# A hybrid encoder layer on one core: the second block product of the gate and up projections by quarter blocks, four products chained in one PSUM bank

## The chip, the cores and the metric

One core of a Trainium2 chip runs the whole layer as one launch. Its five engines work through queues of their own: TensorE (PE, with its weight loads PEld), VectorE (DVE), ScalarE (ACT), GpSimd (POOL) and SyncE (SP, which issues the DMAs). The metric is the device time in microseconds (us), from which the median of several runs is taken.

## The reference, cut to what matters

```python
u = x @ w_in                                  # retention heads, windowed attention heads
h = layer_norm(alpha * x + concat(R, A) @ w_out)
g, up = h @ w_ffn_gate, h @ w_ffn_up          # 1024 x 1024 by 1024 x 2816, twice
ffn = (silu(g) * up) @ w_ffn_down
out = layer_norm(alpha * h + ffn + sigmoid(h @ w_ple_gate) * (p @ w_ple_proj))
```

All of it is float32, and 1024 tokens run through one layer. The change lies in the lines of `g`, `up` and `silu(g) * up`.

## The kernel before, in words

Every float32 operand of a matmul is split into a high and a low part (`split`: ACT rounds, DVE subtracts), and a product is made of three matmuls (`mm3c`, lines 783 to 785: high by high, high by low, low by high).

Gate and up have 22 hidden blocks of 128 columns, taken as 11 pairs. For a pair n, with m = 0 the gate weights and m = 1 the up weights, the 256 hidden columns by 1024 inner by 1024 tokens are a 2 by 2 by 2 block product. It is done with seven products instead of eight (Strassen's scheme in Winograd's form). `RIGHT[p]` holds the token side of product p, ready split; the weight side is loaded as `raw` and `ln` tiles, summed where the scheme asks for it (`s_sums`), and split into an operand tile. A unit is one product p for one m: four steps of the inner size by three matmuls, 12 matmuls of 512 columns, into one bank. A pair has 14 units. The products go to three banks per m: X takes products 1 and 2, Y takes 6, 7 and 4, Z takes 5 and 3. `post` reads the banks and adds up the four output blocks c11, c12, c21 and c22; each has its gate half put through Silu (`finish`, m = 0) and multiplied by its up half (`finish`, m = 1). `asum` then forms the differences of the blocks that the down projection wants, and they are stored in `ad`.

The order on PE, DVE, ACT, POOL and SP is the order in which the code emits it (`manual_schedule`). The loop over the units emits for each the matmuls (`mm`), then `post`, and then `ahead(2, ...)`, which prepares (`prep`) operands for up to 8 units further on. Each engine works off its queue in that order, save that a PE weight load can run beside the matmul before it; an instruction that waits holds back all that stands behind it. In the kernel before, DVE makes the low parts and the sums that read a bank; POOL makes the weight sums (lines 1187 to 1191), the products with the Silu halves (line 1217) and the differences (line 1221). Operand tiles rotate through four tiles `w` and four tiles `u`, the eight PSUM banks through four names (`mm`, `s`, `t`, `o`) of two banks each.

Of the kernel before, what the change touches and what calls it, by code (L numbers as in the profile page):

```python
# [9 lines left out]
F32 = mybir.dt.float32  # L10
# [32 lines left out]
def layer(tc, xT, xn, w_first, w_mt, w_rv, w_out, w_pg, w_pe, pT, w_gu, w_dn,  # L43
# [26 lines left out]
    def split(raw, hi, lo):  # L70
        act.activation(hi, raw, AF.Copy)  # L71
        dve.tensor_tensor(lo, raw, hi.bitcast(F32), ALU.subtract)  # L72
# [699 lines left out]
    def ct(shape, tag, bufs=None, dt=F32):  # L772
        return cpool.tile(list(shape), dt, tag=tag, bufs=bufs, name=nm(tag))
# [7 lines left out]
    def mm3c(o, lh, ll, rh, rl, start, stop):  # L781

        pe.matmul(o, lh, rh, start=start, stop=False, skip_group_check=True)  # L783
        pe.matmul(o, lh, rl, start=False, stop=False, skip_group_check=True)  # L784
        pe.matmul(o, ll, rh, start=False, stop=stop, skip_group_check=True)  # L785
# [375 lines left out]
    sarena = arena8  # L1161
    ptags = ("mm", "s", "t", "o")

    def pair_tile():
        return a_tile([P, 2, HF], "ev")

    stores = []

    class Pair:
# [10 lines left out]
                for j in range(2):  # L1180
                    self.raw[m, i, j] = r[:, j * HF:(j + 1) * HF]

        def s_sums(self, m, part=(0, 1)):
            a = lambda i, j: self.raw[m, i, j]
            s = self.s[m] = [sarena[:, 4 * m + k, :] for k in range(4)]
            if 0 in part:
                pool.tensor_tensor(s[1], a(1, 0), a(1, 1), ALU.add)  # L1187
                pool.tensor_tensor(s[0], s[1], a(0, 0), ALU.subtract)  # L1188
            if 1 in part:
# [3 lines left out]
        def prep(self, p, m, k):  # L1193
            src = {1: lambda: self.raw[m, 0, 0], 2: lambda: self.raw[m, 0, 1], 4: lambda: self.raw[m, 1, 1],
                   5: lambda: self.s[m][1], 6: lambda: self.s[m][0], 7: lambda: self.s[m][2],
                   3: lambda: self.s[m][3]}[p]()
            t = wp.tile([P, 2, HF], F32R, tag="w", bufs=4, name=nm("w")) if k % 2 == 0 else ct([P, 2, HF], "u", 4, F32R)
            split(src, t[:, 0, :], t[:, 1, :])
            self.ops[p, m] = t

        def mm(self, p, m):
            g = {1: 0, 2: 0, 6: 1, 7: 1, 4: 1, 5: 2, 3: 2}[p]
            first = p in (1, 6, 5)
            if first:
                self.bank[g, m] = bank(ptags[(3 * self.n + g) % 4])
            b, w, r = self.bank[g, m], self.ops[p, m], RIGHT[p]
            for kt in range(4):
                c = slice(kt * P, (kt + 1) * P)
                mm3c(b, w[:, 0, c], w[:, 1, c], r[:, 0, kt, :], r[:, 1, kt, :], first and kt == 0, kt == 3)

        def finish(self, name, m):

            c = self.ev[name]
            if m == 0:
                act.activation(c[:, 0, :], c[:, 0, :], AF.Silu)  # L1215
            else:
                pool.tensor_tensor(c[:, 1, :], c[:, 0, :], c[:, 1, :], ALU.mult)  # L1217

        def asum(self, dst, left, right, op):

            pool.tensor_tensor(self.ev[dst][:, 0, :], left, right, op)  # L1221

        def post(self, p, m, k):
            ev, X, Y, Z = self.ev, self.bank.get((0, m)), self.bank.get((1, m)), self.bank.get((2, m))

            def get(name):
                if m == 0:
                    ev[name] = pair_tile()
                return ev[name][:, m, :]

            def add(name, left, right):
                dve.tensor_tensor(get(name), ev[left][:, m, :], right, ALU.add)  # L1232

            a = lambda name: ev[name][:, 1, :]
            s = lambda name: ev[name][:, 0, :]
            wait = 2 if self.n < NP - 1 else 8
            if p == 1:
                act.activation(get("s1"), X, AF.Copy)
            elif p == 6:
                add("u2", "s1", Y)  # L1240
            elif p == 2:
                c = get("c11")
                if m == 0:
                    act.activation(c, X, AF.Silu)
                else:
                    dve.tensor_tensor(c, ev["c11"][:, 0, :], X, ALU.mult)
            elif p == 7:
                add("u3", "s1", Y)
                add("c22", "u3", Z)
                self.finish("c22", m)  # L1250
            elif p == 4:
                add("c21", "s1", Y)
                self.finish("c21", m)
                if m:
                    self.asum("c21", a("c21"), a("c11"), ALU.subtract)
                    stores.append((k + wait, lambda: sp.dma_start(ad[self.n, 2, :, 0, :], s("c21"))))
                    self.asum("c11", s("c21"), a("c22"), ALU.subtract)
                    stores.append((k + wait, lambda: sp.dma_start(ad[self.n, 0], ev["c11"])))
                    self.asum("c22", a("c22"), a("c21"), ALU.subtract)
                    stores.append((k + wait, lambda: sp.dma_start(ad[self.n, 3], ev["c22"])))  # L1260
            elif p == 3:
                add("c12", "u2", Z)
# [9 lines left out]
    def g_unit(n, p, m, k):  # L1272
        pr = pairs2[n]

        def prep():
            if p == 1 and n:
                pr.load(m)
            pr.prep(p, m, k)
            if p == 1:
                if n:  # L1280
                    pr.s_sums(m)
                else:
                    pr.s_sums(m, (0,))
                    if m:
                        pr.s_sums(0, (1,))
                        pr.s_sums(1, (1,))

        return prep, lambda: pr.mm(p, m), lambda: pr.post(p, m, k)
# [323 lines left out]

    ET = mybir.EngineType
    with tc.manual_schedule(engines={ET.PE, ET.DVE, ET.Activation, ET.Pool, ET.SP}):
        ahead(2, 4)
        for k in range(NG):
            gunits[k][1]()
            gunits[k][2]()
            ahead(2, k + 1 + min(8, 4 + k))
# [106 lines left out]
```

## Time and profile before

| what | value |
|---|---|
| runs | 1180.26 us median of 3 (1179.91 to 1180.78) |
| the profiled execution | 1180.62 us, of which the span of the instructions 1178.8 us |
| granted PE clock | 0.997 |
| PE, PEld busy | 99%, 82% of the span |
| DVE, ACT, POOL busy | 65%, 45%, 31% of the span |
| gate and up | from 540 us to about 960 us of the span |

A busy PE in this profile means that a matmul is under way, and matmuls overlap: one of 512 columns is listed with 0.39 us, but the next starts long before that is over. The rate is read from the starts in the timeline. An engine's idle time counts only where it ends in a wait of PE.

### The profile page before, as it was taken

How to read it: one execution, taken by the hardware profiler on the slowest of the kernel's cores; microseconds unless marked ns; L12 is line 12 of the kernel's file. 1: busy time of each engine (PE TensorE's matmuls, PEld its weight loads, DVE VectorE, ACT ScalarE, POOL GpSimd, SP SyncE). 2: the span in 40 equal slices, each digit the busy share in tenths (PEclk: the TensorE clock that was granted, in tenths of full speed). 3: DMA queues.
4: the chain of work that ended last, by engine and by line, in shares of the span. 5: the costliest groups of instructions: out<-in, count | busy, mean ns of one | idle time of the engine just before them, and what ended most of it. 6: DMA issues, size and time to landing. Idle time of an engine off the chain costs nothing.

```text
span 1178.8 us, 17058 instructions
## 1 busy us (share of the span) xinstructions
PE 1167.3 (99%) x6068; PEld 968.4 (82%) x6068; DVE 767.3 (65%) x1310; ACT 534.4 (45%) x1049; POOL 365.5 (31%) x346
## 2 busy tenths in 40 slices
PE   9999999999999999999999999999999999999996
PEld 7888888888888888888788888888888888888885
DVE  5566678776849688948655455545555465774777
ACT  5566348777756265214332333323333325563463
POOL 2001010202010020004765647464655341134242
PEclk9999999999999999999999999999999999999998
DMA  6345656545346955665323331233213179999977
GB/s 253 107 148 215 241 182 240 188 152 205 123 151 240 361 186 195 242 221 176 124 76 120 134 110 70 90 134 135 77 63 129 72 221 323 354 270 229 258 164 208
DMA packets 80661, 211.71 MB, mean 180 GB/s; under 512 B 9536, under 2 KB 14784, under 8 KB 80576
## 3 DMA queue, kind: packets, MB, share of 16 engines
q1 hardware_dynamic: 71936, 193.84, 46.2%
q0 software_dynamic: 8640, 16.78, 8.0%
q8 instruction: 48, 0.79, 0.3%
q14 instruction: 37, 0.30, 0.1%
HBM read 139.29 MB, written 62.13 MB: 171 GB/s over the span
## 4 chain that ended last, share of the span: by engine, by line
PE 94%; DVE 3%; ACT 1%; issue 1%; DMA 1%; DVEq 0%; SPq 0%; ACTq 0%
PE bmm L77 6%; PE bs L785 6%; PE bs L783 6%; PE bs L784 6%; PE bmm L79 6%; PE bmm L78 6%; PE bt L783 5%; PE bt L785 5%; PE bt L784 5%; PE bmm L785 5%; PE bmm L783 5%; PE bmm L784 5%; PE bo L785 5%; PE bo L783 5%; PE bo L784 5%; PE bo L565 2%
## 5 line engine op out<-in xcount | busy, mean ns | idle before, releaser
L77 PE MATMUL bmm<-H,w 128*128 128x512 f32 x240 | 97.2, 405 | 0.2 <-ACT H L71 0.2
L79 PE MATMUL bmm<-H,w 128*128 128x512 f32 x240 | 94.1, 392 | 0.0
L78 PE MATMUL bmm<-H,w 128*128 128x512 f32 x240 | 94.0, 392 | 0.0
L1187 POOL TENSOR_TENSOR H<-ln 128x512 f32<-128x512 f32 x22 | 28.9, 1312 | 180.2 <-ACT w L71 96.1
L1217 POOL TENSOR_TENSOR ev<-ev 128x512 f32<-128x512 f32 x33 | 55.4, 1679 | 90.6 <-DVE ev L1232 63.6
L72 DVE TENSOR_TENSOR w<-H,w 128x512 fp32r<-128x512 f32 x44 | 41.6, 945 | 62.7 <-ACT w L71 62.7
L72 DVE TENSOR_TENSOR w<-raw,w 128x512 fp32r<-128x512 f32 x56 | 46.3, 832 | 47.3 <-ACT w L71 47.1
L526 POOL COPY sc<-skb 128x1 f32<-128x1 f32 x64 | 14.8, 240 | 182.5 <-PE bt L553 162.5
L1215 ACT ACTIVATE ev<-ev 128x512 f32<-128x512 f32 x33 | 20.9, 632 | 103.5 <-DVE ev L1232 103.5
L1221 POOL TENSOR_TENSOR ev<-ev,ev 128x512 f32<-128x512 f32 x44 | 62.7, 1436 | 2.6
L72 DVE TENSOR_TENSOR u<-H,u 128x512 fp32r<-128x512 f32 x47 | 38.0, 809 | 36.6 <-ACT u L71 36.2
L77 PEld LDWEIGHTS bmm<-H,w 128*128 128x128 f32 x240 | 45.1, 188 | 10.3 <-ACT H L71 1.1
L79 PEld LDWEIGHTS bmm<-H,w 128*128 128x128 f32 x240 | 45.0, 188 | 10.0
L78 PEld LDWEIGHTS bmm<-H,w 128*128 128x128 f32 x240 | 45.2, 188 | 7.8
L71 ACT ACTIVATE u<-H 128x512 fp32r<-128x512 f32 x47 | 29.6, 630 | 43.3 <-POOL H L1188 11.1
L535 ACT ACTIVATE sc<-sc,st 128x385 f32<-128x385 f32 (+1 forms) x64 | 37.2, 584 | 17.1 <-DVE st L533 17.0
L71 ACT ACTIVATE w<-raw 128x512 fp32r<-128x512 f32 x56 | 34.5, 623 | 18.8 <-PE bmm L79 6.9
L531 DVE CUSTOM_DVE_ANT_0 sc<-cst,bs,skb 128x384 f32<-128x384 f32 (+1 forms) x64 | 34.9, 577 | 9.2 <-PE bs L530 7.9
L493 POOL TENSOR_TENSOR sm<-sm,cst 128x8 f32<-128x8 f32 x8 | 13.8, 1727 | 79.9 <-DVE sm L492 79.9
L894 POOL TENSOR_TENSOR stt<-stt,cst 128x1 f32<-128x1 f32 x8 | 12.2, 1520 | 83.8 <-DVE stt L893 83.8
L1191 POOL TENSOR_TENSOR H<-raw,H 128x512 f32<-128x512 f32 x22 | 37.3, 1697 | 0.0
L71 ACT ACTIVATE w<-H 128x512 fp32r<-128x512 f32 x44 | 27.3, 621 | 21.0 <-PE bs L785 6.3
(813 smaller groups left out, 3756.2 us busy)
## 6 DMA issues: line engine op xcount, KB each, us to landing
ad<-ev SPq DMA_DIRECT2D x33, 512.0 KB, 2.6
pgd<-pro SPq DMA_DIRECT2D x28, 512.0 KB, 3.0
raw<-in_w_gu SPq DMA_DIRECT2D x22, 512.0 KB, 4.5
ln<-in_w_gu SPq DMA_DIRECT2D x22, 512.0 KB, 3.6
raw<-ad SPq DMA_DIRECT2D x40, 256.0 KB, 5.5
ln<-ad SPq DMA_DIRECT2D x37, 256.0 KB, 6.4
H<-in_w_dn SPq DMA_DIRECT2D x33, 256.0 KB, 6.6
wod<-aq SPq DMA_DIRECT2D x15, 512.0 KB, 2.7
```

The lines of the kernel that those rows point to most:

```text
L71: act.activation(hi, raw, AF.Copy)
L72: dve.tensor_tensor(lo, raw, hi.bitcast(F32), ALU.subtract)
L77: pe.matmul(o, lh, rh, start=start, stop=False)
L78: pe.matmul(o, lh, rl, start=False, stop=False)
L79: recent[0] = pe.matmul(o, ll, rh, start=False, stop=stop).ins.name
L535: act.activation(sc[g][:, :nk + 1], sc[g][:, :nk + 1], AF.Exp, bias=st_[:, 1, j, g:g + 1], accum_out=st_[:, 2, j, g:g + 1])
L783: pe.matmul(o, lh, rh, start=start, stop=False, skip_group_check=True)
L784: pe.matmul(o, lh, rl, start=False, stop=False, skip_group_check=True)
L785: pe.matmul(o, ll, rh, start=False, stop=stop, skip_group_check=True)
L1191: pool.tensor_tensor(s[3], a(0, 1), s[0], ALU.subtract)
L1217: pool.tensor_tensor(c[:, 1, :], c[:, 0, :], c[:, 1, :], ALU.mult)
L1221: pool.tensor_tensor(self.ev[dst][:, 0, :], left, right, op)
```

## The change

From the third pair on (`FROM = 2`), product 2 of both m is no longer two units of 12 matmuls. Its weight side (m by two halves of the inner size) and its token side (`RIGHT[2]`, two halves of the inner size by two halves of 256 tokens) are cut once more, and the product is done as seven quarter products by the same scheme: 7 by 2 by 3 = 42 matmuls of 256 columns instead of 24 of 512. They come in three parts, which the text calls F0 (quarter products 1, 6 and 5), F1 (7 and 2) and F2 (4 and 3), woven between the units of products 1, 6 and 5: (1,0), (1,1), F0, (6,0), F1, (6,1), F2, (5,0), (5,1), (7,0), (7,1), (4,0), (4,1), (3,0), (3,1), where (p,m) is product p for that m. The quarter products share two banks, in halves of 256 columns; `post_fine` has DVE add the halves into c11 after each part, and F1 accumulates on top of halves that F0 wrote. The token side of the quarter products (`fine_right`) is summed and split once, during the first two pairs.

In all pairs, products 1, 6, 7 and 4 now accumulate in one bank W per m, and ACT copies the bank between them (`s1`, `u2`, `u3`; the fourth goes through Silu or a multiplication straight from the bank). The sums `add("u2", ...)`, `add("u3", ...)` and `add("c21", ...)` on DVE are gone. All that POOL computed in this stage, the weight sums, the products with the Silu halves and the differences, stands on DVE. Operand tiles are taken from a list of eight and given back after the matmuls that read them (`take_op`, `free_op`); F0 needs three at once, so `ahead` stops while fewer are free.

```diff
+    Q = HF // 2
+    FINE = ((1, 6, 5), (7, 2), (4, 3))
+    FROM = 2
...
+        def prep(self, p, m):
             a = lambda i, j: self.raw[m, i, j]
-            s = self.s[m] = [sarena[:, 4 * m + k, :] for k in range(4)]
-                pool.tensor_tensor(s[1], a(1, 0), a(1, 1), ALU.add)
-                pool.tensor_tensor(s[0], s[1], a(0, 0), ALU.subtract)
-                pool.tensor_tensor(s[2], a(0, 0), a(1, 0), ALU.subtract)
-                pool.tensor_tensor(s[3], a(0, 1), s[0], ALU.subtract)
...
+            if p == 6:
+                dve.tensor_tensor(s[1], a(1, 0), a(1, 1), ALU.add)
+                dve.tensor_tensor(s[0], s[1], a(0, 0), ALU.subtract)
...
+            t = self.ops[p, m] = take_op()
             split(src, t[:, 0, :], t[:, 1, :])
+            if p == 5:
+                dve.tensor_tensor(s[2], a(0, 0), a(1, 0), ALU.subtract)
+                dve.tensor_tensor(s[3], a(0, 1), s[0], ALU.subtract)
...
+        def mm_fine(self, part):
+            if part == 0:
+                self.fb = [bank(ptags[(3 * self.n + 1) % 4]) for _ in range(2)]
+            for q in FINE[part]:
...
+                for kt in range(2):
+                    c = slice(c0 + kt * P, c0 + (kt + 1) * P)
+                    mm3c(o, t[:, 0, c], t[:, 1, c], hi[:, kt, :], lo[:, kt, :], q in (1, 5) and kt == 0, kt == 1)
...
+        def post_fine(self, part):
...
+            if part == 0:
+                add(c12, v[:, 0, Q:], bx)
+                add(low, v[:, 1, :].rearrange("p (j c) -> p j c", j=2), twice(bx))
+                add(c12, c12, by)
+            elif part == 1:
+                add(low, low, twice(by))
+                add(c22, c22, bz)
+                add(c11, v[:, 0, :Q], bx)
+            else:
+                add(c12, c12, bz)
+                add(c21, c21, bw)
+                self.finish("c11", 0)
+                self.finish("c11", 1)
...
         def mm(self, p, m):
-            g = {1: 0, 2: 0, 6: 1, 7: 1, 4: 1, 5: 2, 3: 2}[p]
-            first = p in (1, 6, 5)
+            g = {1: 0, 6: 0, 7: 0, 4: 0, 2: 1, 5: 2, 3: 2}[p]
+            first = p in (1, 2, 5)
...
         def finish(self, name, m):
...
-                pool.tensor_tensor(c[:, 1, :], c[:, 0, :], c[:, 1, :], ALU.mult)
+                dve.tensor_tensor(c[:, 1, :], c[:, 0, :], c[:, 1, :], ALU.mult)
...
         def asum(self, dst, left, right, op):
-            pool.tensor_tensor(self.ev[dst][:, 0, :], left, right, op)
+            dve.tensor_tensor(self.ev[dst][:, 0, :], left, right, op)
...
             elif p == 6:
-                add("u2", "s1", Y)
+                act.activation(get("u2"), W, AF.Copy)
...
             elif p == 7:
-                add("u3", "s1", Y)
-                add("c22", "u3", Z)
+                act.activation(get("u3"), W, AF.Copy)
+                add("c22", "u3", Z, "u3")
...
-        for p in (1, 6, 5, 2, 7, 4, 3) if n else (1, 2, 6, 5, 7, 4, 3):
+        for p in (1, 6, 5, 7, 4, 3) if n >= FROM else (1, 2, 6, 5, 7, 4, 3):
             for m in range(2):
+                if n >= FROM and p == 6:
+                    gunits.append(f_unit(n, m))
                 gunits.append(g_unit(n, p, m, len(gunits)))
+            if n >= FROM and p == 6:
+                gunits.append(f_unit(n, 2))
...
-        while done[what] < min(upto, len(units)):
+        while done[what] < min(upto, len(units)) and (what < 2 or units[done[2]][3] <= len(oslots)):
```

What moves on DVE is seen at the place where one pair hands over to the next, from the last sums of products 4 and 3 to the first sums of the next pair. The rows below are DVE's queue of the kernel before at that place, in order; each is line, operation, output and inputs, partitions by elements. `ev` tiles hold blocks, a name that starts with `b` is a bank, and line 72 is the low part of an operand.

```order
L1232 TENSOR_TENSOR ev1029_7152<-ev1005_6963,bo1009_6986 128x512
L72 TENSOR_TENSOR w1030_7155<-H697_4542,w1030_7155 128x512
L1232 TENSOR_TENSOR ev1029_7152<-ev1005_6963,bo1012_7004 128x512
L72 TENSOR_TENSOR u1031_7175<-H697_4542,u1031_7175 128x512
L1232 TENSOR_TENSOR ev1032_7190<-ev1010_6999,bt1014_7021 128x512
L72 TENSOR_TENSOR w1033_7193<-raw1019_7067,w1033_7193 128x512
L1232 TENSOR_TENSOR ev1032_7190<-ev1010_6999,bt1016_7037 128x512
L72 TENSOR_TENSOR u1034_7211<-raw1022_7091,u1034_7211 128x512
L72 TENSOR_TENSOR w1037_7232<-H697_4542,w1037_7232 128x512
L72 TENSOR_TENSOR u1039_7249<-H697_4542,u1039_7249 128x512
L1232 TENSOR_TENSOR ev1041_7266<-ev1036_7230,bmm1040_7253 128x512
```

After each unit stood one bank sum and one low part: the two sums of c21, the two of c12, and then the first of the next pair's u2.

The kernel after, DVE, at the same place: from the multiplication of c21 (line 1367, bank `bo883`) on. Line 1335 is `asum`, lines 1227 and 1228 are the weight sums of product 6, line 1243 is a sum of a quarter product, line 1346 a bank sum.

```order
L1367 TENSOR_TENSOR ev829_5336<-ev829_5336,bo883_6741 128x512
L1335 TENSOR_TENSOR ev829_5336<-ev829_5336,ev823_5330 128x512
L1335 TENSOR_TENSOR ev823_5330<-ev829_5336,ev825_5332 128x512
L1335 TENSOR_TENSOR ev825_5332<-ev825_5332,ev829_5336 128x512
L1227 TENSOR_TENSOR H697_4542<-ln887_6819 128x512
L1228 TENSOR_TENSOR H697_4542<-H697_4542,raw882_6739 128x512
L72 TENSOR_TENSOR u811_5318<-H697_4542,u811_5318 128x512
L1243 TENSOR_TENSOR cst_367<-raw882_6739,raw884_6759 128x256
L72 TENSOR_TENSOR u817_5324<-cst_367,u817_5324 128x256
L1346 TENSOR_TENSOR ev824_5331<-ev824_5331,bs889_6858 128x512
L1227 TENSOR_TENSOR H697_4542<-ln888_6823 128x512
L1228 TENSOR_TENSOR H697_4542<-H697_4542,raw884_6759 128x512
```

Eight operations now stand between the multiplication that follows unit (4,1) and the sum that follows unit (3,0), where one low part stood between two bank sums before.

The kernel after, DVE, further on in the same hand-over, after seven rows that are left out here: from the low part of operand (5,0) to the three sums after F0 (line 1295, bank `bo895`).

```order
L72 TENSOR_TENSOR w814_5321<-H697_4542,w814_5321 128x512
L1234 TENSOR_TENSOR H697_4542<-raw882_6739,ln887_6819 128x512
L1235 TENSOR_TENSOR H697_4542<-raw882_6739,H697_4542 128x512
L72 TENSOR_TENSOR u815_5322<-H697_4542,u815_5322 128x512
L1234 TENSOR_TENSOR H697_4542<-raw884_6759,ln888_6823 128x512
L1235 TENSOR_TENSOR H697_4542<-raw884_6759,H697_4542 128x512
L1295 TENSOR_TENSOR ev827_5334<-ev826_5333,bo895_7044 128x256
L1295 TENSOR_TENSOR ev827_5334<-ev826_5333,bo895_7044 128x512
L1295 TENSOR_TENSOR ev827_5334<-ev827_5334,bo895_7044 128x256
```

The weight sums for products 7 and 3 (lines 1234 and 1235) stand ahead of the sums of F0, which F1 on PE waits for.

More of the change, by code (lines that the diff above doesn't have):

```diff
@@ L1162, in layer, with take_op, free_op, fine_right @@
     ptags = ("mm", "s", "t", "o")
-    def pair_tile():
-        return a_tile([P, 2, HF], "ev")
+    Q = HF // 2
+    FINE = ((1, 6, 5), (7, 2), (4, 3))
+    FROM = 2
+    evs, nev = [], [0]
+    oslots = []
+    fright, fsum = {}, []
+    def pair_tile():
+        nev[0] += 1
+        return evs[(nev[0] - 1) % len(evs)]
+    def take_op():
+        return oslots.pop(0)
+    def free_op(t):
+        oslots.append(t)
+    def fine_right(R):
+        x = cst[:, 0:HF].rearrange("p (k c) -> p k c", k=2)
+        def blk(i, j, part):
+            return R[:, part, 2 * i:2 * i + 2, j * Q:(j + 1) * Q]
+        def both(left, right):
+            dve.tensor_tensor(x, blk(*left, 0).bitcast(F32), blk(*right, 0).bitcast(F32), ALU.subtract)
+            dve.tensor_tensor(x, x, blk(*left, 1).bitcast(F32), ALU.add)
+            dve.tensor_tensor(x, x, blk(*right, 1).bitcast(F32), ALU.subtract)
+        def less(left):
+            dve.tensor_tensor(x, blk(*left, 0).bitcast(F32), x, ALU.subtract)
+            dve.tensor_tensor(x, x, blk(*left, 1).bitcast(F32), ALU.add)
+        for q, (i, j) in {1: (0, 0), 2: (1, 0), 3: (1, 1)}.items():
+            fright[q] = blk(i, j, 0), blk(i, j, 1)
+        other = a_tile([P, 2, 2, Q], "fine", dt=F32R)
+        fright[7] = other[:, 0], other[:, 1]
+        fright[5] = tuple(ct([P, 2, Q], "sg", 2, F32R) for _ in range(2))
+        fright[6] = tuple(ct([P, 2, Q], "p", 2, F32R) for _ in range(2))
+        fright[4] = blk(0, 1, 0), blk(0, 1, 1)
+        return [lambda: (both((1, 1), (0, 1)), split(x, *fright[7])), lambda: (both((0, 1), (0, 0)), split(x, *fright[5])),
+                lambda: (less((1, 1)), split(x, *fright[6])), lambda: (less((1, 0)), split(x, *fright[4]))]
     stores = []
@@ L1193, in prep @@
[L1193 to L1197, printed above, removed]
-            split(src, t[:, 0, :], t[:, 1, :])
-            self.ops[p, m] = t
+            s = self.s.setdefault(m, [sarena[:, 4 * m + k, :] for k in range(4)])
@@ new lines, in prep_fine, with sum_, put @@
+        def prep_fine(self, part):
+            x, y = (self.raw[m, 0, 1] for m in range(2))
+            left = {1: x[:, :Q], 2: x[:, Q:], 4: y[:, Q:], 5: fsum[0], 6: fsum[1], 7: fsum[2], 3: fsum[3]}
+            def sum_(q, a, b, op):
+                dve.tensor_tensor(left[q], a, b, op)
+            def put(t, h, q):
+                c = slice(h * Q, (h + 1) * Q)
+                split(left[q], t[:, 0, c], t[:, 1, c])
+                self.fine[q] = t, h * Q
+            if part == 0:
+                self.fine = {}
+                t, u, v = (take_op() for _ in range(3))
+                self.fu = u
+                sum_(5, y[:, :Q], y[:, Q:], ALU.add)
+                sum_(6, left[5], x[:, :Q], ALU.subtract)
+                split(x, t[:, 0, :], t[:, 1, :])
+                self.fine.update({1: (t, 0), 2: (t, Q)})
+                put(u, 0, 5)
+                put(v, 0, 6)
+            elif part == 1:
+                sum_(7, x[:, :Q], y[:, :Q], ALU.subtract)
+                put(self.fu, 1, 7)
+            else:
+                w = take_op()
+                sum_(3, x[:, Q:], left[6], ALU.subtract)
+                put(w, 0, 4)
+                put(w, 1, 3)
@@ new lines, in mm_fine @@
+        def mm_fine(self, part):
+            if part == 0:
+                self.fb = [bank(ptags[(3 * self.n + 1) % 4]) for _ in range(2)]
+            for q in FINE[part]:
+                t, c0 = self.fine[q]
+                i, j = {1: (0, 0), 2: (0, 0), 6: (0, 1), 7: (0, 1), 5: (1, 0), 3: (1, 0), 4: (1, 1)}[q]
+                o = self.fb[i][:, j * Q:(j + 1) * Q]
+                hi, lo = fright[q]
+                for kt in range(2):
+                    c = slice(c0 + kt * P, c0 + (kt + 1) * P)
+                    mm3c(o, t[:, 0, c], t[:, 1, c], hi[:, kt, :], lo[:, kt, :], q in (1, 5) and kt == 0, kt == 1)
+            for q in ((6,), (7, 2), (4,))[part]:
+                free_op(self.fine[q][0])
@@ new lines, in post_fine, with add, twice @@
+        def post_fine(self, part):
+            ev = self.ev
+            if part == 0:
+                ev["c11"] = pair_tile()
+            o, v = ev["c11"], ev["s1"]
+            (c11, c12), (c21, c22) = ([o[:, m, j * Q:(j + 1) * Q] for j in range(2)] for m in range(2))
+            (bx, by), (bz, bw) = ([b[:, j * Q:(j + 1) * Q] for j in range(2)] for b in self.fb)
+            low = o[:, 1, :].rearrange("p (j c) -> p j c", j=2)
+            def add(out_, x, y):
+                dve.tensor_tensor(out_, x, y, ALU.add)
+            def twice(b):
+                return b.unsqueeze(1).to_broadcast([P, 2, Q])
+            if part == 0:
+                add(c12, v[:, 0, Q:], bx)
+                add(low, v[:, 1, :].rearrange("p (j c) -> p j c", j=2), twice(bx))
+                add(c12, c12, by)
+            elif part == 1:
+                add(low, low, twice(by))
+                add(c22, c22, bz)
+                add(c11, v[:, 0, :Q], bx)
+            else:
+                add(c12, c12, bz)
+                add(c21, c21, bw)
+                self.finish("c11", 0)
+                self.finish("c11", 1)
@@ L1261, in post @@
             elif p == 3:
-                add("c12", "u2", Z)
+                add("c12", "u2", Z, "u2")
                 self.finish("c12", m)
@@ L1275, in prep, with f_unit @@
         def prep():
[L1276 to L1288, printed above, removed]
+            pr.prep(p, m)
+            if n + 1 < NP and p in (5, 4):
+                pairs2[n + 1].load(m, ((0,), (1,))[p == 4])
+        return prep, lambda: pr.mm(p, m), lambda: pr.post(p, m, k), 1
+    def f_unit(n, part):
+        pr = pairs2[n]
+        return lambda: pr.prep_fine(part), lambda: pr.mm_fine(part), lambda: pr.post_fine(part), (3, 0, 1)[part]
     for n in range(NP):
-        for p in (1, 6, 5, 2, 7, 4, 3) if n else (1, 2, 6, 5, 7, 4, 3):
+        for p in (1, 6, 5, 7, 4, 3) if n >= FROM else (1, 2, 6, 5, 7, 4, 3):
             for m in range(2):
+                if n >= FROM and p == 6:
+                    gunits.append(f_unit(n, m))
                 gunits.append(g_unit(n, p, m, len(gunits)))
+            if n >= FROM and p == 6:
+                gunits.append(f_unit(n, 2))
     LASTS = [(0, 1, "mm"), (1, 1, "s"), (2, 1, "mm"), (3, 1, "s"), (4, 1, "mm"), (4, 0, "s"), (5, 1, "mm"), (5, 0, "s"),
@@ L1614, in layer @@
     with tc.manual_schedule(engines={ET.PE, ET.DVE, ET.Activation, ET.Pool, ET.SP}):
+        for _ in range(4):
+            oslots.append(wp.tile([P, 2, HF], F32R, tag="w", bufs=4, name=nm("w")))
+            oslots.append(ct([P, 2, HF], "u", 4, F32R))
+        fine = fine_right(RIGHT[2])
+        evs.extend(a_tile([P, 2, HF], "ev") for _ in range(7))
+        fsum.extend([cst[:, 0:Q], cst[:, Q:2 * Q], cst[:, 2 * Q:3 * Q], ct([P, Q], "fs", 1)])
         ahead(2, 4)
```

37 lines of the change are left out of this document (19 added, 18 removed).

## The prediction

> **What bounds the kernel now.** I read the page first, for the shares and the chain that ended last:
>
> ```profile
> span 1178.8 us, 17058 instructions
> ...
> PE 1167.3 (99%) x6068; PEld 968.4 (82%) x6068; DVE 767.3 (65%) x1310; ACT 534.4 (45%) x1049; POOL 365.5 (31%) x346
> ...
> PE 94%; DVE 3%; ACT 1%; issue 1%; DMA 1%; DVEq 0%; SPq 0%; ACTq 0%
> ```
>
> PE is busy almost throughout, and the chain runs through PE. The waits of PE tell whether it ever stood still for gate and up. The columns are who waited for whom, us in total, times, longest:
>
> ```profile
> PE bs L783 <- DVE ev L1232: 0.7, 1, 0.7
> ```
>
> One wait of 0.7 us belongs to this stage (it lies at 570 us). A stretch in the middle of the stage, by windows (busy us and instructions of PE, PEld, DVE, ACT, POOL, then the granted clock):
>
> ```profile
> 650.00:700.00 50.00, 50.00 (x222) 41.39 (x222) 27.23 (x33) 15.97 (x28) 31.35 (x21) 1.00 0.30 110
> ```
>
> PE never idles, DVE is busy for 27 us of 50, POOL for 31. So the stage ends when PE has issued its matmuls; the other engines have slack, and the reader should note how much of DVE's slack the change uses.
>
> The rate of PE comes from the starts in its timeline (start, duration). Fourteen steps of 512 columns lie between these two rows:
>
> ```profile
> 699.69 0.39 PE L785 MATMUL bs<-H,w 128*128 128x512 f32 x1
> ...
> 702.87 0.39 PE L784 MATMUL bs<-H,u 128*128 128x512 f32 x1
> ```
>
> (702.87 - 699.69) / 14 = 0.227 us for each. A unit of 12 is 2.73 us, a pair of 14 units 38.15 us.
>
> **The change on PE.** No matmul of 256 columns stands in this stage, but some in attention:
>
> ```profile
> 330.36 0.28 PE L530 MATMUL bs<-kz,aq 128*128 128x256 f32 x1
> 330.47 0.28 PE L529 MATMUL bs<-k,aq 128*128 128x256 f32 x1
> 330.59 0.28 PE L530 MATMUL bs<-kz,aq 128*128 128x256 f32 x1
> 330.71 0.39 PE L77 MATMUL bmm<-H,w 128*128 128x512 f32 x1
> ```
>
> Three steps take 0.35 us, 0.117 us each. 24 matmuls of 0.227 (5.45 us) become 42 of 0.117 (4.91 us): 0.54 us a pair, 4.9 us over the nine pairs. [...]
>
> So an unhindered pair is 12 units and 42 quarter matmuls, 32.7 + 4.9 = 37.6 us.
>
> **The change on DVE.** What an operation costs there, from its timeline:
>
> ```profile
> 553.23 1.78 DVE L72 TENSOR_TENSOR w<-H,w 128x512 fp32r<-128x512 f32 x1
> 554.94 0.68 DVE L72 TENSOR_TENSOR u<-H,u 128x512 fp32r<-128x512 f32 x1
> ...
> 560.34 0.68 DVE L72 TENSOR_TENSOR u<-H,u 128x512 fp32r<-128x512 f32 x1
> ...
> 566.14 0.67 DVE L1232 TENSOR_TENSOR ev<-ev,bs 128x512 f32<-128x512 f32 x1
> 566.85 0.69 DVE L1232 TENSOR_TENSOR ev<-ev,bmm 128x512 f32<-128x512 f32 x1
> ```
> ```profile
> 551.00:554.90 3.90, 3.85 (x17) 2.87 (x16) 3.90 (x3) 2.90 (x6) 3.47 (x3) 1.00 0.72 164
> 554.90:560.90 6.00, 6.00 (x29) 4.95 (x28) 6.00 (x11) 1.35 (x3) 0.00 (x0) 1.00 0.35 102
> ```
>
> The nine steps from 554.94 to 560.34, through a full queue with POOL still (0.00 in the second window), are 0.60 us each. At 553.23 POOL computes too (3.47 of 3.90), and one takes 1.78. Where an operation reads what the one before it wrote (the last two rows), the step is 0.71. POOL gives up these:
>
> ```profile
> L1187 POOL TENSOR_TENSOR H<-ln 128x512 f32<-128x512 f32 x22 | 28.9, 1312 | 180.2 <-ACT w L71 96.1
> L1217 POOL TENSOR_TENSOR ev<-ev 128x512 f32<-128x512 f32 x33 | 55.4, 1679 | 90.6 <-DVE ev L1232 63.6
> L1221 POOL TENSOR_TENSOR ev<-ev,ev 128x512 f32<-128x512 f32 x44 | 62.7, 1436 | 2.6
> ```
>
> With three more lines of weight sums like the first they are 15 operations a pair. On DVE each costs 0.60 instead of 1.3 to 1.7 us, and the contention of 1.78 goes. Half-width rows, for the quarter products, with ACT's beside it:
>
> ```profile
> L431 DVE COPY kv<-bt 128x256 f32<-128x256 f32 x4 | 1.7, 425 | 3.7 <-PE bt L423 3.7
> L429 ACT ACTIVATE kv<-bt 128x256 f32<-128x256 f32 x4 | 1.5, 372 | 0.5 <-DVE kv L431 0.5
> ```
>
> A half-width DVE step is then about 0.34 us (0.425 less the 0.08 by which a full one overlaps the next). A pair's DVE queue grows from 25 operations to 35 full and 15 half: 35 x 0.60 + 15 x 0.34 = 26.1 us of 37.6, 69%. On average it fits. It doesn't fit where it is bunched.
>
> **The hand-over.** Count from the moment at which PE has issued unit (4,1) and starts (3,0). Until F1 of the next pair, PE has (3,0), (3,1), (1,0), (1,1), F0 and (6,0): five units and 18 quarter matmuls, 13.6 + 2.1 = 15.7 us. F1 adds onto halves of a bank that the three sums after F0 must have read. In the queue of DVE these stand behind everything in the order rows of the change. What a hand-over between engines costs:
>
> ```profile
> 701.73 0.39 PE L785 MATMUL bs<-H,w 128*128 128x512 f32 x1
> 702.16 0.69 DVE L1232 TENSOR_TENSOR ev<-ev,bs 128x512 f32<-128x512 f32 x1 [0.88 <-PE bs L785]
> 702.88 0.69 DVE L72 TENSOR_TENSOR w<-ln,w 128x512 fp32r<-128x512 f32 x1
> 696.72 0.60 ACT L1238 ACTIVATE ev<-bt 128x512 f32<-128x512 f32 x1 [2.03 <-PE bt L785]
> 697.22 0.62 ACT L71 ACTIVATE w<-H 128x512 fp32r<-128x512 f32 x1
> 697.87 1.32 DVE L72 TENSOR_TENSOR w<-H,w 128x512 fp32r<-128x512 f32 x1 [1.76 <-ACT w L71]
> ```
>
> PE's last matmul starts at 701.73, DVE goes on at 702.16: 0.43 later, 0.2 us after the start of the next unit. ACT's rounding ends at 697.84, the subtraction starts 0.03 later. So a weight sum that is split at once holds DVE for 0.69 + 0.03 + 0.62 + 0.03 = 1.37 us before the low part can start. Walking down DVE's queue (start of the next operation, us):
>
> - c21 times up, three differences, the two weight sums of (6,0): 0.2 + 3 x 0.72 + 2 x 0.60 + 1.37 = 4.9
> - low part, the sum and low part of quarter product 7, with ACT's half-width 0.37 between: 0.60 + 0.85 + 0.45, to 6.8
> - c12 after (3,0), the sums of (6,1), low part: 0.60 + 0.72 + 1.37 + 0.60, to 10.1
> - c12 after (3,1), its multiplication, a difference: 0.72 + 0.72 + 0.60, to 12.2
> - F2's sum and low parts: 0.85, to 13.0; then 1.17 in which ACT copies s1 and rounds (5,0), to 14.2
> - low parts and weight sums of (5,0) and (5,1): 4 x 0.60 + 2 x 0.72 = 3.8, to 18.0
> - the three sums after F0: 0.34 + 0.60 + 0.46, to 19.4
>
> (0.72 also where an operation waits for more than one engine, as the low part at 702.88, 0.72 after the sum ahead of it.) PE reaches F1 at 15.7 and waits until 19.4: 3.7 us a pair. Of it about 0.6 falls ahead of (6,0), since ACT, held up behind DVE's sum for F2, copies s1 only by 13.6 where F0 ends at 13.0; that is inside the 3.7, not beside it.
>
> After F1 nothing is late: F1, (6,1), F2 and six units are 1.4 + 2.7 + 1.4 + 16.4 = 21.9 us, in which DVE has some 20 operations, about 11 us, and is idle before the next (4,1). The four products in one bank cost nothing there: (4,0) waits for the copy after (7,0), with a whole unit of 2.73 us as cover against a 0.60 copy. If that cover went, it would be 0.8 us for each copy. The period is 19.4 + 21.9 = 41.3 us against 38.15: 3.15 more, and nine pairs have such a hand-over ahead of them (the third to the eleventh): 28 us.
>
> **Unseen prices.** The stretch's lower end: all steps 0.60, nine of 0.12 less, and ACT's waits 0.3 shorter: 18.0. Upper end: 0.12 more on eleven steps, as where waits double: 20.7. That is 1.7 to 4.4 us a pair, 16 to 40 in all; I take the middle, since the steps are known one by one. The first two pairs have no quarter products, so F1's wait doesn't exist there: between -0.7 (the old wait at 570 us goes) and +3.7 (one such stretch); I take 0. The extra sums of `fine_right` lie in these pairs, under 4 us each, on a DVE otherwise 57% busy (36 x 0.60 of 38.15). The down projection starts with POOL free and DVE idle: 0, within 1 us.
>
> **Sum.** The profiled execution took 1180.6 us, of which the span is 1178.8 us. 1180.6 + 28 = 1208.6; the median of the runs is 0.4 lower, so 1208.
>
> **The rivals.** (A) Faster: DVE clears the hand-over in time, and only PE's saving is left: 1180.3 - 4.9 = 1175.4. It decides at a stretch of 15.7 + 0.5 = 16.2 us or less. For it: DVE's average of 69%. Against: 28 operations in 16.2 us would need 0.58 each with no wait for ACT, and the rows show 0.60 and five such waits. (B) PE's clock falls in each wait. The first matmuls show what a slow start costs:
>
> ```profile
> 1.31 3.59 PE L142 MATMUL bo<-sq 128*128 128x512 bf16 x8 [1.31 <-POOL sq L139]
> ```
>
> Eight in 3.59 us, 0.45 each, half the later rate. If every wait of PE brought that back for as long, it would cost half of 3.6, 1.8 us, nine times 16: 1224. No row shows an idle time of PE over 1.3 us in the middle, so the trace can't exclude it. [...] (C) The quarter matmuls run no faster than a weight load is long:
>
> ```profile
> 330.24 0.19 PEld L530 LDWEIGHTS bs<-kz,aq 128*128 128x128 f32 x1
> 330.36 0.19 PEld L529 LDWEIGHTS bs<-k,aq 128*128 128x128 f32 x1
> ```
>
> 0.19 instead of 0.117 on the 24 of F1 and F2 (F0's lie inside the wait): 1.75 a pair, 16 in all: 1224. Against it: the loads start 0.12 apart, though in a run of four only. (D) The bunch is milder, because waits overlap more than I count: a stretch of 17, PE waits 1.3, the pair costs 0.75 more: 1187.
>
> **How the numbers follow.** The forecast with its own range (1196 to 1220) has 0.70, D 0.10, A 0.06, B 0.08, C 0.04, no change 0.02. The range 1191 to 1224 takes in the forecast, the upper half of D and the near side of B and C, leaving out about 0.15. A measurement of this kernel tells 0.2% (2.4 us) from no change. Faster by more: 0.06 (A); within: 0.03; slower by more: 0.91.
>
> **What would show it.** Right: PE's waits name the first matmul of F1 (line 783) behind DVE's line 1295, nine times about 3 us, and ACT's copy (line 1352) nine times under 1 us; DVE back to back from (4,1) to F0's sums; DVE's steps near 0.60. Wrong: no such wait and a total near 1175 (A); starts 0.45 apart after the waits (B); quarter matmuls 0.19 apart (C); or PE's waits at (4,0), at the copies of the chained bank.

## The result, and the profile after

The changed kernel takes 1213.6 us (median of 4 runs, 1212.1 to 1217.3) against 1180.1; the ratio is 1.0288, interval 1.0262 to 1.0313. The profiled execution took 1212.4 us, its span is 1210.6, 31.8 us more than before. The forecast was 1208, with a range of 1191 to 1224.

The page of the changed kernel, in the lines that were shown of the one before: PE is listed as busy for 4.5 us more, and the chain now runs through DVE for 12% of the span instead of 3%.

```profile
span 1210.6 us, 17418 instructions
...
PE 1171.8 (97%) x6230; PEld 975.4 (81%) x6230; DVE 844.7 (70%) x1571; ACT 570.6 (47%) x1133; POOL 120.2 (10%) x181
...
PE 82%; DVE 12%; ACT 3%; issue 2%; DMA 0%; ACTq 0%; DVEq 0%; SPq 0%
```

PE's waits of the changed kernel between 600 and 1000 us (us in total, times, longest). Line 1295 is the sums after a part of the quarter products, line 1352 ACT's copy s1:

```profile
PE bo L783 <- DVE ev L1295: 7.4, 3, 2.5
PE bmm L783 <- DVE ev L1295: 5.0, 2, 2.5
PE bs L783 <- DVE ev L1295: 5.0, 2, 2.5
PE bt L783 <- DVE ev L1295: 5.0, 2, 2.5
PE bmm L783 <- ACT ev L1352: 1.9, 3, 0.7
PE bo L783 <- ACT ev L1352: 1.3, 2, 0.6
PE bt L783 <- ACT ev L1352: 1.3, 2, 0.6
PE bs L783 <- ACT ev L1352: 1.3, 2, 0.6
```

Nine waits of 2.5 us for DVE and nine of 0.6 for ACT, and no others: the nine hand-overs. The first of them in PE's timeline (start, duration; in brackets the idle time ahead and what ended it):

```profile
610.82 0.39 PE L783 MATMUL bs<-h,w 128*128 128x512 f32 x1
...
623.73 0.28 PE L785 MATMUL bo<-sg,u 128*128 128x256 f32 x1
624.65 0.50 PE L783 MATMUL bmm<-H,u 128*128 128x512 f32 x1 [0.63 <-ACT ev L1352]
...
627.31 0.39 PE L785 MATMUL bmm<-H,u 128*128 128x512 f32 x1
630.16 0.39 PE L783 MATMUL bo<-fine,u 128*128 128x256 f32 x1 [2.46 <-DVE ev L1295]
```

(3,0) starts at 610.82, F1 at 630.16: a stretch of 19.34 us, where the walk gave 19.4. DVE's timeline over the same stretch, in excerpts:

```profile
611.02 0.69 DVE L1367 TENSOR_TENSOR ev<-ev,bo 128x512 f32<-128x512 f32 x1
611.74 2.02 DVE L1335 TENSOR_TENSOR ev<-ev,ev 128x512 f32<-128x512 f32 x3
...
614.40 0.69 DVE L1228 TENSOR_TENSOR H<-H,raw 128x512 f32<-128x512 f32 x1
615.87 0.69 DVE L72 TENSOR_TENSOR u<-H,u 128x512 fp32r<-128x512 f32 x1 [0.78 <-ACT u L71]
...
628.76 1.34 DVE L1295 TENSOR_TENSOR ev<-ev,bo 128x256 f32<-128x256 f32 x3
```

The sum and its low part stand 1.47 us apart at 614.40 and 615.87 (ACT's rounding lies between), the queue ends with the sums after F0 at 630.10, and F1 follows 0.06 later.

A pair's period is read from PE's starts of unit (1,0). Of the changed kernel, four of them, the third to the sixth pair's:

```profile
616.26 0.39 PE L783 MATMUL bmm<-h0a,w 128*128 128x512 f32 x1
657.67 0.39 PE L783 MATMUL bs<-h0a,w 128*128 128x512 f32 x1
699.06 0.39 PE L783 MATMUL bt<-h0a,w 128*128 128x512 f32 x1
742.05 0.39 PE L783 MATMUL bo<-h0a,w 128*128 128x512 f32 x1
```

The periods are 41.41, 41.39 and 42.99 us. Before it was 38.08 for each:

```profile
617.64 0.39 PE L783 MATMUL bmm<-h0a,w 128*128 128x512 f32 x1
655.72 0.39 PE L783 MATMUL bs<-h0a,w 128*128 128x512 f32 x1
```

The third period is 1.6 us longer because of the clock. Windows of the changed kernel (busy us and instructions of PE, PEld, DVE, ACT, POOL, then the granted clock), two pairs of neighbours:

```profile
710.90:714.31 3.41, 1.35 (x11) 1.35 (x12) 3.21 (x7) 1.27 (x3) 0.00 (x0) 1.00 0.92 196
714.31:717.72 3.41, 3.41 (x11) 2.74 (x11) 2.64 (x5) 0.86 (x2) 0.00 (x0) 0.50 0.74 259
919.11:922.52 3.41, 1.54 (x7) 0.94 (x5) 3.41 (x7) 1.86 (x3) 0.00 (x0) 1.00 0.35 103
922.52:925.93 3.41, 2.82 (x18) 2.60 (x19) 2.78 (x7) 1.26 (x2) 0.00 (x0) 1.00 0.79 209
```

After the wait at 710 us the clock was granted at 0.50 for 3.41 us; after the one at 920 it stayed at 1.00. Two of the nine waits were followed by a half clock; the second began at 881.57 us, 167.25 us after the first at 714.31, which is 49 times 3.413. The account closes: nine pairs at 41.40 - 38.08 = 3.32 are 29.9 us, two half clocks 3.2, and the first pair is 1.3 us shorter than before (38.10 instead of 39.44): 31.8.

### The profile page after: what moved, and what is told of

It is laid out like the page before. It is cut to its first block, busy times and chain, and to the rows that moved or that the text cites. A ratio compares the mean times of both kernels' runs of the same rounds, so it can differ in the third digit from the quotient of the medians.

```text
span 1210.6 us, 17418 instructions
## 1 busy us (share of the span) xinstructions
PE 1171.8 (97%) x6230; PEld 975.4 (81%) x6230; DVE 844.7 (70%) x1571; ACT 570.6 (47%) x1133; POOL 120.2 (10%) x181
## 4 chain that ended last, share of the span: by engine, by line
PE 82%; DVE 12%; ACT 3%; issue 2%; DMA 0%; ACTq 0%; DVEq 0%; SPq 0%
PE bmm L77 6%; PE bmm L79 6%; PE bmm L78 6%; PE bt L783 5%; PE bt L785 5%; PE bt L784 5%; PE bmm L783 4%; PE bmm L785 4%; PE bmm L784 4%; PE bs L783 4%; PE bs L785 4%; PE bs L784 4%; PE bo L783 4%; PE bo L785 4%; PE bo L784 4%; DVE ev L1335 2%
## 5 line engine op out<-in xcount | busy, mean ns | idle before, releaser
L1472 POOL DMA_DIRECT2D h0b<-in_w_dn x24 | 21.6, 902 | 576.5 <-DVE h0a L72 543.9
L72 DVE TENSOR_TENSOR w<-H,w 128x512 fp32r<-128x512 f32 x48 | 33.1, 690 | 31.9 <-ACT w L71 31.9
L72 DVE TENSOR_TENSOR w<-raw,w 128x512 fp32r<-128x512 f32 x52 | 35.7, 692 | 24.4 <-ACT w L71 24.2
L71 ACT ACTIVATE w<-H 128x512 fp32r<-128x512 f32 x48 | 30.1, 627 | 36.0 <-DVE H L1228 33.3
L72 DVE TENSOR_TENSOR u<-H,u 128x512 fp32r<-128x512 f32 x43 | 29.5, 686 | 9.4 <-ACT u L71 9.4
L72 DVE TENSOR_TENSOR u<-raw,u 128x512 fp32r<-128x512 f32 (+1 forms) x30 | 18.3, 608 | 25.4 <-ACT u L71 25.4
L541 ACT ACTIVATE sc<-sc,st 128x384 f32<-128x384 f32 (+1 forms) x64 | 34.0, 580 | 0.8 <-DVE st L539 0.8
L71 ACT ACTIVATE H<-ln 128x512 fp32r<-128x512 f32 (+1 forms) x34 | 22.9, 677 | 24.1 <-DMA ln<-ad 7.5
L526 POOL COPY sc<-skb 128x1 f32<-128x1 f32 x64 | 15.7, 253 | 182.1 <-PE bt L553 157.2
L72 DVE TENSOR_TENSOR H<-ln,H 128x512 fp32r<-128x512 f32 (+1 forms) x34 | 25.0, 746 | 8.4 <-ACT H L71 8.3
L1335 DVE TENSOR_TENSOR ev<-ev,ev 128x512 f32<-128x512 f32 x44 | 29.5, 690 | 1.1
```

The source lines that it names most:

```text
L541: behind(act.activation(sc[g][:, :nk], sc[g][:, :nk], AF.Copy, scale=st_[:, 3, j, g:g + 1]))
L1335: dve.tensor_tensor(self.ev[dst][:, 0, :], left, right, op)
```

## The experiments

**The change without its quarter products.** The token side of product 2 is still summed in place as the change does it, so product 2 computes with other data here.

```diff
-    FROM = 2
+    FROM = NHID
```

> The change without its quarter products (product 2 stays two units of 12 matmuls in all pairs); the chained bank, ACT's copies and DVE's taking over of POOL's work remain. Theory (F1 waits for DVE's queue at the hand-over): without F1 nothing on PE waits for DVE's sums after a hand-over, so PE never stands still in this stage; the pairs take the old 38.1 us, and the total is 1180.1 less the 1.3 us that the first pair gains in the changed kernel, 1178.8. Rival 1 (the chained bank makes PE wait for ACT's copies): waits of PE for the copy (line 1352 or 1354), up to 0.6 us in each of ten pairs, 1185. Rival 2 (the load on DVE alone, wherever it stands, costs): DVE's steps or its share hold PE back and the total stays near 1205.

1180.0 us, ratio 1.000 (0.999 to 1.0009). PE has no wait in this stage, and a pair takes 38.1 us with DVE at 23.5 of them:

```profile
617.10:655.20 38.10, 38.10 (x169) 31.54 (x168) 23.45 (x37) 14.15 (x24) 0.00 (x0) 1.00 0.29 104
```

So neither the chained bank nor the move from POOL to DVE costs anything that shows by itself (the interval is 1.1 us to either side), and rival 1 falls. Rival 2 falls for this load of DVE; a load as in the changed kernel, about 28 us a pair, stands in the last run below. The total misses the expected 1178.8 by 1.2 us. The first pair does take 38.10 us instead of 39.44, but the stage began 0.83 us later in this execution (540.95 instead of 540.12), and the median shows no gain. In the traces of this case the stage begins anywhere from 539.9 to 541.8 us.

**The sums for products 7 and 3 behind those of F0.**

```diff
+            if p == 7 and m == 0:
+                for i in range(2):
+                    dve.tensor_tensor(sarena[:, 4 * i + 2, :], self.raw[i, 0, 0], self.raw[i, 1, 0], ALU.subtract)
...
-            if p == 5:
-                dve.tensor_tensor(s[2], a(0, 0), a(1, 0), ALU.subtract)
+            if p == 4:
                 dve.tensor_tensor(s[3], a(0, 1), s[0], ALU.subtract)
...
-            if n + 1 < NP and p in (5, 4):
-                pairs2[n + 1].load(m, ((0,), (1,))[p == 4])
+            if n + 1 < NP and p == 4:
+                pairs2[n + 1].load(m)
```

> Of the changed kernel, the four weight sums for products 7 and 3 (lines 1234, 1235) are moved in DVE's queue from ahead of F0's three sums to behind them: the two for product 7 to the preparation of unit (7,0), the two for product 3 to that of units (4,0) and (4,1); the loads of the next pair that they hold up move with them. Same operations, same count. Theory: four steps of 0.60 us leave the stretch, 19.3 becomes 16.9 us, F1's wait falls from 2.5 us to about 0.1 to 0.4, nine times 2.2 us less; no half clock after so short a wait (3 to 5 us in the runs); in all about 1188, with a new wait at F2 of up to 1 us as the risk (1197). Rival (the stretch is not DVE's queue but latency between engines, or DVE's load in all): the wait stays near 2.5 us and the total near 1213.

1193.7 us, ratio 1.0113 (1.0096 to 1.013). PE's waits between 600 and 1000 us, one row of each sort:

```profile
PE bmm L783 <- ACT ev L1354: 1.9, 3, 0.6
PE bo L783 <- DVE ev L1297: 1.5, 3, 0.5
```

F1's wait falls from 2.46 to 0.5 us by four operations put elsewhere in the same queue, with the same count, and no half clock shows (0.998 granted in all four runs). The period is 39.38 us. It is DVE's queue, not its load. The total misses the 1188 by 6 us. A pair gains 2.02 us instead of 2.2, since a low part ahead of F0's sums now waits 0.31 us for ACT: 1.6 us in all. The first pair takes 2.8 us more than in the changed kernel: a rounding on ACT waited 2.71 us for a moved load, held up the copies behind it, and PE waited 2.1 us for them. Where the remaining 1 to 2 us lie stays open.

**POOL's products and differences back on POOL.**

```diff
-                dve.tensor_tensor(c[:, 1, :], c[:, 0, :], c[:, 1, :], ALU.mult)
+                pool.tensor_tensor(c[:, 1, :], c[:, 0, :], c[:, 1, :], ALU.mult)
...
-            dve.tensor_tensor(self.ev[dst][:, 0, :], left, right, op)
+            pool.tensor_tensor(self.ev[dst][:, 0, :], left, right, op)
```

> Of the changed kernel, the products with the Silu halves and the differences of the blocks are put back on POOL, as they were before; the rest stays. Theory A (what counts is the length of DVE's queue at the hand-over): five operations leave the stretch, 3.3 us, F1's wait goes and the total is about 1186. Theory B (POOL's operations slow DVE's while both read SBUF, 1.78 us against 0.68 in the profile of before): POOL works about 7 us in the stretch, and DVE loses there a good part or all of what it is spared; steps of 1.2 to 1.8 us show on DVE, F1 still waits 1 to 4 us, the total is 1200 to 1225.

1228.0 us in one run, profiled. Two rows of DVE's groups, one of PE's waits, and the starts of (3,0) and of F1 in one hand-over:

```profile
L72 DVE TENSOR_TENSOR u<-raw,u 128x256 fp32r<-128x256 f32 x9 | 13.7, 1519 | 0.0
L1243 DVE TENSOR_TENSOR cst<-raw,raw 128x256 f32<-128x256 f32 x9 | 13.5, 1505 | 0.0
```
```profile
PE bo L783 <- DVE ev L1295: 10.3, 3, 3.4
```
```profile
655.48 0.39 PE L783 MATMUL bt<-h,w 128*128 128x512 f32 x1
...
674.84 0.39 PE L783 MATMUL bmm<-fine,u 128*128 128x256 f32 x1 [3.42 <-DVE ev L1295]
```

Half-width operations that take 0.42 us in the changed kernel take 1.5 beside POOL. What DVE is spared it loses again: the stretch from (3,0) to F1 stays at 19.36 us. ACT's wait goes, and F1's grows to 3.4 us. The granted clock averaged 0.95 between 600 and 1000 us (0.982 over the run), by my estimate about twelve times 3.41 us at half clock for the nine waits. The nine pairs take 389.8 us instead of 375.8, which makes 14 of the 15.7 us by which this run lies above the changed kernel's profiled one; in the other 1.7 the stage began later. Theory B holds for the waits and the slow steps; the total lies 3 us above its 1200 to 1225, and the clock is what it had left out.

**Two sums more ahead of F0's.**

```diff
             if p == 5:
                 dve.tensor_tensor(s[2], a(0, 0), a(1, 0), ALU.subtract)
                 dve.tensor_tensor(s[3], a(0, 1), s[0], ALU.subtract)
+                if self.n >= FROM:
+                    dve.tensor_tensor(s[2], a(0, 0), a(1, 0), ALU.subtract)
```

> Of the changed kernel, the weight sum for product 7 is computed a second time for each m, ahead of F0's sums: two more steps on DVE in each of the nine hand-overs. Theory: F1's wait grows by 2 x 0.60 us in each, from 2.5 to 3.7, nine times 1.2 is 11 us. The clock: in the changed kernel's profile it was halved for 3.41 us after two of the nine waits, those of which one fixed 3.41 us window held the largest idle part (1.99 and 2.06 us of 3.41; 1.87 did not). If a part of about 57% of a window is the limit, then nearly all nine waits of 3.7 us will be followed by a half clock, 1.6 us each, 11 us more than two of them: 1235. If a window has to be idle as a whole, none or one is: 1223.

1235.3 us in one run. F1's wait, and windows around a wait that was followed by a half clock (the first two) and one that was not (the last three):

```profile
PE bs L783 <- DVE ev L1297: 7.4, 2, 3.7
```
```profile
672.17:675.58 3.41, 1.46 (x7) 0.88 (x5) 3.41 (x7) 1.12 (x2) 0.00 (x0) 1.00 0.26 30
675.58:678.99 3.41, 1.66 (x7) 1.66 (x8) 2.90 (x6) 0.77 (x2) 0.00 (x0) 0.50 0.84 215
849.66:853.07 3.41, 1.50 (x7) 0.92 (x5) 3.41 (x7) 1.12 (x2) 0.00 (x0) 1.00 0.18 30
853.07:856.48 3.41, 1.62 (x13) 1.62 (x14) 2.94 (x6) 1.26 (x3) 0.00 (x0) 1.00 0.86 203
856.48:859.89 3.41, 3.41 (x20) 2.92 (x19) 2.64 (x5) 1.18 (x3) 0.00 (x0) 1.00 0.80 249
```

The wait grew by 1.2 us, 0.6 for each operation, as the walk has it. The granted clock averaged 0.96 between 600 and 1000 us (0.984 over the run), by my estimate about ten times 3.41 us at half clock, though not every wait brought one. Here PE idle for 1.95 us of a window of 3.41 (3.41 - 1.46) was followed by one, and idle for 1.91 (3.41 - 1.50) was not. The run with POOL put back has a window with 1.90 us idle (3.41 - 1.51) that was followed by one:

```profile
672.94:676.35 3.41, 1.51 (x12) 1.51 (x13) 3.05 (x6) 1.20 (x2) 0.00 (x0) 1.00 0.70 179
676.35:679.76 3.41, 3.41 (x10) 2.69 (x9) 2.64 (x5) 0.69 (x2) 0.00 (x0) 0.50 0.86 284
```

So half clocks in these runs came after some 1.9 us of idle time in a window, about 56% of it, and since the ends of matmuls in a profile are modelled, it can't be told more finely. A window idle as a whole was not needed.

**F1's wait filled with matmuls that nothing reads.**

```diff
+            if part == 1:
+                for d in [bank(ptags[(3 * self.n + 2) % 4]) for _ in range(2)]:
+                    for _ in range(5):
+                        pe.matmul(d, RIGHT[5][:, 0, 0, 0:P], RIGHT[5][:, 0, 1, :], start=True, stop=True, skip_group_check=True)
             for q in FINE[part]:
```

> The changed kernel with ten matmuls of 512 columns more on PE just ahead of each F1, into a bank that is free there; nothing reads them. They run while PE waits anyway (10 x 0.227 = 2.3 us in a wait of 2.5). Theory: F1 starts no later, since DVE decides; PE's idle time is 0.2 us where it was 2.5, so the clock is never halved; the total is the changed kernel's without its half clocks: the profiled 1212.4 less two of 1.6, 1209, and the runs lie within 1 us of each other instead of 5. Rival (the half clock has another cause, such as the load of the quarter products): half clocks still show, 1212 or more.

1210.0 us (1209.0 to 1211.9), the profiled run 1209.0, ratio 1.0253 (1.0239 to 1.0267). Its period was 41.4 us in every pair, as in the changed kernel where the clock was whole, and F1's wait is down to the 0.2 us of this row:

```profile
PE bs L783 <- DVE ev L1299: 0.4, 2, 0.2
```

More work on PE made the kernel faster: the half clock is gone in all four runs (0.997 to 0.998 granted, as in the kernel before, against 0.991 to 0.995 in the changed kernel). A half clock of 3.41 us takes 0.0014 off the mean over 1210 us, so by this estimate 0.995 to 0.991 means two to five of them, which is enough for the spread from 1212 to 1217. The runs did not lie within 1 us of each other; their 2.9 us are as wide as the kernel before's in the same session.

**The sum of quarter product 3 one unit earlier.**

```diff
             elif part == 1:
                 sum_(7, x[:, :Q], y[:, :Q], ALU.subtract)
+                sum_(3, x[:, Q:], left[6], ALU.subtract)
                 put(self.fu, 1, 7)
             else:
                 w = take_op()
-                sum_(3, x[:, Q:], left[6], ALU.subtract)
```

> Of the changed kernel, the sum of quarter product 3 is made with that of quarter product 7, one unit earlier; nothing else moves. ACT then needn't wait for it ahead of its copy s1, so PE's wait of 0.63 us at (6,0) goes. Theory (both waits lie inside one stretch that DVE's queue sets): F1's wait grows, from 2.46 to about 2.7 us, since PE arrives 0.63 earlier, while the stretch loses only what DVE waited there for ACT (0.2 + 0.6 us): 0.8 us a pair, 7 in all, about 1205 and somewhat more half clocks than two, up to 1212. Rival (the two waits add up, each by itself): F1's wait stays at 2.46 or falls, the pair gains 0.63 to 1.4 us.

1205.1 us in one run, at a granted clock of 0.991, which by the same estimate is five half clocks. PE's wait for the copy is gone, and F1's has become shorter:

```profile
PE bs L783 <- DVE ev L1295: 4.2, 2, 2.1
```

2.1 us, not 2.7: by its numbers this is the rival's result. But the stretch lost 1.3 us, not 0.8 (18.04 instead of 19.34). That the total came out at the expected 1205 is luck: nine times 0.5 us more gained were made up by three more half clocks. DVE's timeline shows the part I had left out; the sum now stands in a gap in which DVE had waited 0.49 us for ACT:

```profile
739.78 0.42 DVE L1243 TENSOR_TENSOR cst<-raw,raw 128x256 f32<-128x256 f32 x1
740.12 0.42 DVE L1243 TENSOR_TENSOR fs<-raw,cst 128x256 f32<-128x256 f32 x1
740.69 0.43 DVE L72 TENSOR_TENSOR w<-cst,w 128x256 fp32r<-128x256 f32 x1
```

F1 still starts 0.06 us after DVE's queue ends, so one stretch with both waits in it still describes it, but the rival's numbers fit as well. A run made to remove only ACT's wait and leave DVE's stretch alone is missing. The run with POOL put back comes to the same, though, and speaks for the one stretch: there ACT's wait is gone, DVE's stretch is as long as in the changed kernel (19.36 and 19.34 us), and F1's wait has grown from 2.46 to 3.42, by what PE no longer loses ahead of (6,0).

**The hand-over cleared.**

```diff
+        def sums6(self, m):
+            a = lambda i, j: self.raw[m, i, j]
+            s = self.s.setdefault(m, [sarena[:, 4 * m + k, :] for k in range(4)])
+            dve.tensor_tensor(s[1], a(1, 0), a(1, 1), ALU.add)
+            dve.tensor_tensor(s[0], s[1], a(0, 0), ALU.subtract)
...
-            if p == 6:
-                dve.tensor_tensor(s[1], a(1, 0), a(1, 1), ALU.add)
-                dve.tensor_tensor(s[0], s[1], a(0, 0), ALU.subtract)
+            if p == 6 and self.n < FROM:
+                self.sums6(m)
...
+                if FROM <= self.n + 1 < NP:
+                    pairs2[self.n + 1].sums6(m)
```

The last two lines stand after `finish("c22", m)`; the sums for products 7 and 3 and for quarter product 3 are moved as in the two runs above, from the third pair on.

> The changed kernel with the hand-over cleared, from the third pair on: the weight sums of products 7 and 3 come after F0's sums, the two of product 6 of the next pair are made in the units (7,0) and (7,1) of the pair before, where DVE is idle, and the sum of quarter product 3 with that of 7. The same operations, at other places. Theory: the stretch falls from 19.3 to about 12 us, under the 15.7 of PE; no wait of PE is left, no half clock; a pair takes 12 x 2.72 + 42 x 0.120 = 37.7 us instead of 38.1; with the 1.3 us of the first pair 1180.1 - 1.3 - 3.4 = 1175.4. Rival (quarter products cost more than their starts show, for instance a restart of 0.1 us in each part): 1177 to 1180.

1176.8 us (1176.3 to 1177.4, 6 runs) against 1180.0; ratio 0.997 (0.9958 to 0.9982). It is faster than both kernels; against the one before it gains 0.3%. Two starts of (1,0), and the window of that pair:

```profile
617.53 0.39 PE L783 MATMUL bmm<-h0a,w 128*128 128x512 f32 x1
655.27 0.39 PE L783 MATMUL bs<-h0a,w 128*128 128x512 f32 x1
```
```profile
617.50:655.30 37.80, 37.80 (x188) 32.09 (x187) 27.85 (x50) 15.18 (x29) 0.00 (x0) 1.00 0.28 106
```

The period is 37.74 us, 0.34 less than before, with DVE busy for 27.85 us of it and no wait of PE: the same arithmetic as in the changed kernel. The quarter products are worth 9 x 0.34 = 3.1 us by the periods. Against the run without quarter products (1180.0 us), whose first pair takes 38.10 us too, the median measures 3.2. The period came out as expected, so the rival of hidden restarts falls; the total misses the expected 1175.4 by 1.4 us, because the first pair's 1.3 us show no more in this total than in that run's. Why they don't stays open.

## Why the prediction was right, and where it was off

**The step that carried it held.** One stretch per pair, from (4,1) to F1, is set by DVE's queue: forecast 19.4 us, measured 19.34; period forecast 41.3, measured 41.40. DVE's steps of 0.60, and of 0.72 where one waits, were met. Not every price was: with a rounding between, the step was 1.47 and 1.48 us, not 1.37, and the operations for (5,0) and (5,1) stood 0.60 us apart throughout, where two were taken at 0.72. These errors, 0.2 us each, cancel, so that the stretch is right to 0.06 us is in part luck. ACT's wait of 0.6 us and F1's of about 3 were named, and measured at 0.63 and 2.46; PE needs 15.78 us for the stretch where nothing waits (from 612.09 to 627.87 in the last run), so it was late by 3.56 us, where 3.7 was forecast. Some 0.3 us of this that the two waits don't show are a matter of counting, since the last matmul before each wait is listed 0.16 us longer than the distance to a next one; about 0.1 is a slower restart (after the wait at 624.65 the next matmul starts 0.34 later instead of 0.23).

**PE's saving was a little smaller.** Quarter matmuls stand 0.120 us apart, not 0.117, and the pair takes 37.74 us instead of 37.6.

**Rival B was not a rival but a part.** I gave the clock a chance of 0.08 and all or nothing, 16 us. It happened after two of nine waits in the profile, 3.2 us. The profiled 1212.4 lies 3.8 above the sum of 1208.6: 3.2 for the half clocks and 1.9 for a pair's 3.32 instead of 3.15 and the rounding to 28, less the first pair's 1.3. The median lies higher still, since two of the other runs were granted less (0.991 and 0.994 against 0.995). The 0.08 was my estimate, and no trace of before showed that waits of up to 3 us leave the clock whole. In the changed kernel's profile the half clock lasts 3.41 us, and 1.99 us of idle time in a window of that length were followed by it; in the run with POOL put back 1.90 were. The length of the wait alone did not decide: of nine waits of 2.5 us two were followed by a half clock, with 2.06 and 1.99 us idle in the 3.41 ahead of it, and the one at 920 us, with 1.87 idle in its window, was not.

**A, C and D did not come.** PE waited in all nine hand-overs; the quarter matmuls ran at 0.120 and not at 0.19 over 18 in a row; the stretch was not 17. The first pair's gain, for which I took 0 and at most 0.7, was 1.3 us in the profile.

## What to carry to other kernels

A queue that is busy for 28.1 us of 41.4 can still hold the bounding engine back, while the same queue, busy for 27.9 of 37.8 in the last run, does not: take the stretch between two things that the bounding engine waits for, walk the other engine's queue through it instruction by instruction, and compare the two sums. What helped here was moving nine operations per pair to a place where the same engine was idle, not taking work off it. If the engine that takes work over slows the one it is to relieve while both work, as POOL does DVE here (1.5 us instead of 0.42), what is handed over may come back as slower steps.

## What the runs showed of the hardware

In the changed kernel's profile the granted PE clock went from 1.00 to 0.50 for 3.41 us at a time, twice, and the two starts lie 167.25 us apart, 49 times 3.413. Read in windows of 3.41 us that lie on this grid, PE was idle for 2.06 and 1.99 us of the two windows ahead of a half clock, and for 1.87 us or less of all others between 600 and 1000 us. In windows of the other runs a half clock followed 1.95 us idle (two sums more) and 1.90 (POOL put back), and none followed 1.91 (two sums more). In the changed kernel the pair with the half clock in it took 1.6 us longer (42.99 us against 41.40). Ten matmuls whose results nobody reads, put into the wait, took F1's wait from 2.5 to 0.2 us, the granted clock from between 0.991 and 0.995 to 0.997 and more, and 3.6 us off the median.
